# Thresholded attention on one core: two banks of a PSUM tile declared independent, and the tail's zero products in other shapes

## The chip, the core and the metric

The kernel runs on one core of a Trainium2 chip. The core has a matrix engine (PE in the profile; PEld is its loading of weights), a vector engine (DVE), an activation engine (ACT), a general engine (POOL) and a queue engine (SP) that issues DMAs. Each engine takes its instructions in the order of the program and waits on semaphores for the others. The metric is the time of one execution in device microseconds; lower is better. The median of three runs of the kernel before is 236.16 us (234.34 to 236.63).

## The reference

Q, K and V have 8 batches of 12 heads, 512 rows and 64 columns, in float32; the threshold is 0.1.

```python
scale = 1.0 / np.sqrt(Q.shape[-1])
scores = np.einsum('bhqd,bhkd->bhqk', Q, K) * scale
weights = np.exp(scores - np.max(scores, axis=-1, keepdims=True))
weights = weights / (np.sum(weights, axis=-1, keepdims=True) + 1e-10)
weights = np.where(weights > threshold, weights, 0)
weights = weights / (np.sum(weights, axis=-1, keepdims=True) + 1e-10)
return np.einsum('bhqk,bhkd->bhqd', weights, V)
```

A row of the output is zero unless one of its 512 softmax weights is above 0.1, which few rows have.

## The kernel before, in words

The kernel fills the output with zeros, looks for the rows that can have a weight above the threshold, and computes only those exactly. The 96 heads go as 48 pairs, and two pairs make a quad (24 quads, numbered q).

**The screening, for each quad.** K and Q are loaded (lines 363 to 372). PE transposes K in float32 (`do_ktr`, line 399) into two PSUM banks, and ACT or DVE copies them to SBUF (`do_kev`, lines 353 and 355); POOL casts the copy to f16 (`do_kh`, line 357). Q is cast by POOL (`do_qcast`), transposed by PE (`do_qtr`, line 425) and copied by DVE (`do_qev`, line 355). Then, for each pair of heads and each of four blocks of 128 keys, `do_sc` (line 452) makes two products, one for each head, each 128 keys by 512 queries, each filling one PSUM bank. `do_ex` turns them into f16 exponentials in SBUF: on ACT (line 461) or by a bit trick on DVE (line 463). An exponential of 512 columns takes one bank; where both banks of a pair lie side by side and one engine does both, one instruction of 1024 columns takes the two. `do_sm` (lines 483 and 494) adds the exponentials up by products with mostly zero weights, four at a time on four column groups of PE, into a PSUM bank of its own, `sum`. `do_bits` (ACT line 442, DVE line 444) and `do_norms` (line 508) do the like for the squares of Q and K, which a bound of the error needs.

**The exact part, for each of four groups of pairs** (16, 16, 12 and 4 pairs) and in seven parts x: DVE picks up to 8 candidates a row (`y`, `d`, `fl`, `mx`, `m`), PE and DVE turn them into row numbers (`ix` line 559, `qi` line 563, `qf` line 567), POOL gathers the rows of Q (`gq`), PE brings them in place (`xm` line 578), DVE masks them (`xev` lines 585 and 588), PE multiplies them with K (`xqk` line 596), ACT takes exponentials (`xexp` line 601), DVE tests them, POOL gathers a row of V (`gv`) and scatters it to the output.

**The tail.** After the last scores PE has the norms of quads 12 to 23 left (their sums go to a bank called `late`), the exact parts 4, 5 and 6, and 44 steps named `spare` (`do_spare`, line 385): products of zeros whose results nobody reads. At the very end the checks are reduced by DVE, PE and DVE (lines 802, 811 to 815), and every engine branches on one number: were a bound broken, a slow exact loop would run (line 821 on), which doesn't happen here.

**The banks.** Seven PSUM banks, numbered 0 to 6, make the ring `one`. They are allotted as three tiles of two banks each and one of one bank:

```python
banks = [psum.tile([P, min(2, pools["one"] - i), S], f32, name=f"one{i}") for i in range(0, pools["one"], 2)]
one = [banks[i // 2][:, i % 2, :] for i in range(pools["one"])]
```

So banks 0 and 1 are one tile, 2 and 3, 4 and 5, and bank 6 is alone. The framework derives the waits between engines from which instruction touched which tile before. The function `sides` gives an instruction one bank or both banks of a tile.

**The order.** `Plan.order` walks a table written out by hand, `ORDER`: one word for each of the 1395 steps, a number and a letter for its engine. For each step it takes banks (and other buffers) from the front of a list of idle ones, traces its instructions, and puts what it gives back at the end of the list. The order on each engine is therefore fixed; only the waits move. The costs and due times in the calls of `add` would serve a planner that is used when the table is empty. The steps of the tail that matter here stand at lines 730 to 736: `spare` takes a bank at its first step and gives it back at its last.

The lines that the change and the prediction touch are 351 to 357 (`copy`), 380 to 385, 391 to 433, 447 to 466, 497 to 509, 531 to 534, 557 to 602 and 730 to 736.

Of the kernel before, what the change touches and what calls it, by code (L numbers as in the profile page):

```python
# [117 lines left out]
def kernel(  # L118
# [20 lines left out]
    P = 128  # L139
# [211 lines left out]
    def copy(eng, dst, src):  # L351
        if eng == "ACT":
            nc.scalar.copy(dst, src)  # L353
        elif eng == "DVE":
            nc.vector.tensor_copy(dst, src)  # L355
        else:
            nc.gpsimd.tensor_copy(dst, src)  # L357

    def issuer(eng):
        return nc.scalar if eng == "ACTQ" else nc.sync  # L360

# [18 lines left out]
    def do_spare(eng, j):  # L380

        dst = one[at("one", "spare")]
        for c, k, m in (((0, P, 32), (32, P, 32), (64, P, 32), (96, P, 32)), ((0, D, P),),
                        ((0, D, 32), (32, D, 32), (64, D, 32), (96, D, 32)), ((0, D, P),))[j % 4]:
            nc.tensor.matmul(dst[c:c + m, :], lhsT=blank[0:k, 0:m], rhs=blank[0:k, :], start=True, stop=True)  # L385
# [5 lines left out]
    def do_ktr(eng, u):  # L391
        q, n0, k = u
        src, dst = k_b[at("k", q)], [one[at("one", ("ktr", u, i))] for i in range(2)]
        for n in range(k):
            for r in range(SO):
                for i in range(2):
                    ps = slice(i * D, (i + 1) * D)
                    c = (n * SO + r) * D
                    nc.tensor.matmul(dst[i][:, c:c + D], lhsT=src[ps, n0 + n, r, :],  # L399
                                     rhs=identity_f32[ps, ps], is_transpose=True, start=True, stop=True)  # L400
# [5 lines left out]

    def do_kev(eng, u, i, both):
# [4 lines left out]
        copy(eng, dst, src)  # L412
# [4 lines left out]
    def do_qtr(eng, u):  # L417
        q, n0, k = u
        src, dst = qh_b[at("qh", q)], [one[at("one", ("qtr", u, i))][:].bitcast(f16) for i in range(2)]
        for n in range(k):  # L420
            for r in range(SO):
                for i in range(2):
                    ps = slice(i * D, (i + 1) * D)
                    c = (n * SO + r) * D
                    nc.tensor.matmul(dst[i][:, c:c + D], lhsT=src[ps, n0 + n, r, :], rhs=identity_h[ps, ps],  # L425
                                     is_transpose=True, start=True, stop=True)

    def do_qev(eng, u, i, both):
# [4 lines left out]
        copy(eng, dst, src)  # L433
# [13 lines left out]
    def do_sc(eng, hp, t):  # L447
        q, n = divmod(hp, 2)
        qk = qk_b[at("qk", q)]
        for h in range(2):  # L450
            ps = slice(h * D, (h + 1) * D)
            nc.tensor.matmul(one[at("one", ("sc", hp, t, h))][:], lhsT=qk[ps, 1, n, t * P:(t + 1) * P], rhs=qk[ps, 0, n, :],  # L452
                             start=True, stop=True)
# [3 lines left out]
    def do_ex(eng, hp, t, h, both):  # L457
        src = sides(("sc", hp, t), h, both)
        dst = e_b[at("e", (hp, t))][:, 0 if both else h:2 if both else h + 1, :]
        if eng == "ACT":  # L460
            nc.scalar.activation(dst, src, ACTF.Exp, scale=scale, bias=-11.0 * math.log(2.0))  # L461
        else:
            nc.vector.tensor_scalar(dst.bitcast(u16), src, scale * LOG2E * 1024.0, 4096.0,  # L463
                                    op0=ALU.mult, op1=ALU.add)
# [32 lines left out]
    def do_norms(eng, q):  # L497
# [8 lines left out]
        for j in range(4):  # L506
            w = w_1 if squared[q, j // 2] else w_n
            nc.tensor.matmul(dst[32 * j:32 * j + 32, :], lhsT=w[:, c:c + 32], rhs=v[:, j // 2, j % 2, :],  # L508
# [384 lines left out]
```

## Time and profile before

| | |
|---|---|
| Runs (us) | 236.63, 234.34, 236.16; median 236.16 |
| The profiled execution | 234.87 us, of which the span from the first instruction to the last is 233.1 us |
| Busy share of the span | PE 79%, ACT 72%, DVE 64%, POOL 38% |
| Mean granted TensorE clock | 0.949 |

The profile is of one execution. A row of groups gives the line of the code, the engine, the operation, what is written and read (buffer numbers left out), the count, then busy time and mean duration of one, then the idle time of the engine before it and what ended it. In the view of waits, "DVE e L463 <- ACT e L461: 9.5, 12, 1.4" reads: before instructions of line 463 DVE sat idle for 9.5 us in 12 stretches, the longest 1.4 us, and what ended them was ACT's line 461. In the timeline a row has start and duration in us; instructions of one kind behind each other are merged ("x4"), and the idle time of the engine before stands in brackets. Matmuls are pipelined and their recorded durations include their way through the array, so that PE's busy share is not its load.

### The profile page before, as it was taken

Reading aid. Unit: us, or ns where it says so; the run is one execution under the profiler, and the core shown is the slowest. Engines: PE = TensorE matmul, PEld = TensorE weight load, DVE = VectorE, ACT = ScalarE, POOL = GpSimd, SP = SyncE. Lnnn points to the kernel's source line nnn. Section 1 sums busy time; section 2 is a strip of 40 time slices with the busy share of each in tenths; the row PEclk is TensorE's granted clock in tenths of the full one; section 3 lists DMA queues with packets and bytes.
Section 4 is the critical chain, followed back from the end, with each engine's and each line's share of the span. In section 5 each row is a group of like instructions: output and inputs, shape, how many; then the busy total and the mean of one; then the engine's idle time right before and its main releaser. Section 6 shows DMA issues by size and latency. Waiting matters only on the chain.

```text
span 233.1 us, 6162 instructions
## 1 busy us (share of the span) xinstructions
PE 184.4 (79%) x2434; PEld 71.8 (31%) x2434; DVE 150.3 (64%) x319; ACT 167.5 (72%) x242; POOL 87.8 (38%) x169
## 2 busy tenths in 40 slices
PE   6597689867687987797989798737897787798993
PEld 2233233413232333242433234311423223532220
DVE  6435478757768877686798677562585678676411
ACT  3655569757678898869889779755595989987730
POOL 4631725334133244306152532850350680323530
PEclk9979679979999999999999999976999999999997
DMA  6999760975897079708985898999920000000000
GB/s 171 271 276 293 168 180 13 275 198 151 249 284 193 3 222 239 262 3 217 300 251 143 214 321 229 247 271 379 403 115 3 0 5 0 5 6 2 6 2 6
DMA packets 70608, 38.32 MB, mean 164 GB/s; under 512 B 52020, under 2 KB 64429, under 8 KB 70576
## 3 DMA queue, kind: packets, MB, share of 16 engines
q1 hardware_dynamic: 68832, 37.10, 56.3%
q10 hardware_dynamic: 1072, 0.66, 1.0%
q8 instruction: 20, 0.33, 0.5%
q0 software_dynamic: 672, 0.13, 0.4%
q14 instruction: 12, 0.10, 0.1%
HBM read 25.62 MB, written 12.81 MB: 165 GB/s over the span
## 4 chain that ended last, share of the span: by engine, by line
PE 46%; DVE 25%; ACT 20%; issue 6%; DMA 2%; ACTq 0%; DVEq 0%
ACT e L461 17%; DVE e L463 14%; PE one L452 14%; PE sum L494 9%; PE one L385 6%; PE one L399 4%; PE one L596 4%; DVE qk L355 4%; DVE kt L355 3%; PE one L377 2%; ACT kt L353 2%; PE one L425 2%; DMA k<-in_K_dram 2%; PE sum L483 2%; PE one L508 1%
## 5 line engine op out<-in xcount | busy, mean ns | idle before, releaser
L461 ACT ACTIVATE e<-one 128x512 f16<-128x512 f32 (+1 forms) x181 | 129.4, 779 | 34.7 <-PE one L452 23.7
L463 DVE TENSOR_SCALAR e<-one 128x512 uint16<-128x512 f32 (+1 forms) x110 | 82.8, 778 | 37.7 <-PE one L452 20.8
L452 PE MATMUL one<-qk 64*128 64x512 f16 x384 | 71.3, 398 | 26.5 <-DVE e L463 14.5
L357 POOL CAST qk<-kt 128x512 f16<-128x512 f32 x46 | 28.2, 628 | 88.4 <-ACT kt L353 64.9
L494 PE MATMUL sum<-e,w_s 128*32 128x512 f16 x704 | 54.9, 400 | 2.0 <-DVE d L537 1.3
L452 PEld LDWEIGHTS <-qk 64*128 64x128 f16 x384 | 21.0, 96 | 71.2 <-issue 68.3
L357 POOL CAST qh<-q 128x512 f16<-128x512 f32 x47 | 27.7, 613 | 5.1 <-DMA q<-in_Q_dram 4.7
L353 ACT COPY kt<-one 128x512 f32<-128x512 f32 (+1 forms) x25 | 16.0, 656 | 10.5 <-DVE kt L355 5.9
L494 PEld LDWEIGHTS <-w_s 128*32 128x32 f16 x704 | 14.4, 97 | 28.6 <-issue 22.6
L399 PE MATMUL one<-identity_f,k 64*128 64x64 f32 x384 | 17.7, 234 | 6.2 <-ACT e L461 4.2
L355 DVE COPY qk<-one 128x1024 f16<-128x1024 f16 (+2 forms) x33 | 17.3, 542 | 7.3 <-PE one L425 3.0
L399 PEld LDWEIGHTS one<-identity_f,k 64*128 64x128 f32 x384 | 15.3, 144 | 12.7 <-ACT e L461 7.4
L355 DVE COPY kt<-one 128x512 f32<-128x512 f32 (+1 forms) x18 | 12.7, 717 | 9.5 <-PE one L399 6.2
L442 ACT ACTIVATE v<-qk 128x1024 bf16<-128x1024 f16 x16 | 15.9, 1047 | 2.0 <-PE one L508 2.0
L571 POOL DMA_INDIRECT qs<-in_Q_dram,idx x7 | 7.8, 1112 | 24.9 <-DVE idx L563 16.6
L385 PE MATMUL one<-blank 128*32 128x512 bf16 (+2 forms) x110 | 14.9, 386 | 0.5 <-DVE ix L567 0.5
L444 DVE TENSOR_SCALAR v<-qk 128x512 int32<-128x512 int32 x32 | 12.8, 429 | 1.6 <-PE sum L508 1.6
L425 PE MATMUL one<-identity_h,qh 64*128 64x64 f16 x384 | 10.0, 191 | 4.2 <-ACT e L461 2.0
L596 PE MATMUL one<-kt,xq 128*32 128x512 f32 x96 | 11.7, 598 | 2.0 <-ACT e L461 1.4
L425 PEld LDWEIGHTS <-qh 64*128 64x128 f16 x384 | 8.6, 95 | 10.8 <-issue 7.8
L377 PE MATMUL one<-blank,w_n 128*32 128x512 bf16 x104 | 9.3, 471 | 3.2 <-ACT e L461 1.6
L622 POOL DMA_INDIRECT vr<-in_V_dram,idx x7 | 7.7, 1104 | 7.5 <-PE one L425 4.4
(98 smaller groups left out, 103.2 us busy)
## 6 DMA issues: line engine op xcount, KB each, us to landing
out_dram<-zero SPq DMA_DIRECT2D x24, 512.0 KB
k<-in_K_dram SPq DMA_DIRECT2D x95, 128.0 KB
q<-in_Q_dram SPq DMA_DIRECT2D x23, 512.0 KB
q<-in_Q_dram ACTq DMA_DIRECT2D x2, 256.0 KB
k<-in_K_dram ACTq DMA_DIRECT2D x1, 128.0 KB
qs<-in_Q_dram,idx POOLq DMA_INDIRECT x7, 3.3
vr<-in_V_dram,idx POOLq DMA_INDIRECT x7, 3.1
out_dram<-vr,idx POOLq DMA_INDIRECT x7, 3.0
```

The lines of the kernel that those rows point to most:

```text
L353: nc.scalar.copy(dst, src)
L355: nc.vector.tensor_copy(dst, src)
L357: nc.gpsimd.tensor_copy(dst, src)
L385: nc.tensor.matmul(dst[c:c + m, :], lhsT=blank[0:k, 0:m], rhs=blank[0:k, :], start=True, stop=True)
L399: nc.tensor.matmul(dst[i][:, c:c + D], lhsT=src[ps, n0 + n, r, :], rhs=identity_f32[ps, ps], is_transpose=True, start=True, stop=True)
L425: nc.tensor.matmul(dst[i][:, c:c + D], lhsT=src[ps, n0 + n, r, :], rhs=identity_h[ps, ps], is_transpose=True, start=True, stop=True)
L442: nc.scalar.activation(dst, src, ACTF.Square)
L452: nc.tensor.matmul(one[at("one", ("sc", hp, t, h))][:], lhsT=qk[ps, 1, n, t * P:(t + 1) * P], rhs=qk[ps, 0, n, :], start=True, stop=True)
L461: nc.scalar.activation(dst, src, ACTF.Exp, scale=scale, bias=-11.0 * math.log(2.0))
L463: nc.vector.tensor_scalar(dst.bitcast(u16), src, scale * LOG2E * 1024.0, 4096.0, op0=ALU.mult, op1=ALU.add)
L494: nc.tensor.matmul(dst[32 * j:32 * j + 32, :], lhsT=w, rhs=x, start=first, stop=False, skip_group_check=True)
L596: nc.tensor.matmul(one[at("one", ("xs", x))][sl, :], lhsT=xq_b[at("xq", x)][:, n, sl], rhs=kt_b[at("kt", hp // 2)][:, hp % 2, :], start=(n ...
```

## The change

`copy` returns its instruction. A new list `users` holds, for each PSUM tile, the instructions that used it with their kind and banks. `uses` is called with every score, transpose, exponential, copy out of PSUM, zero product, late norm and product of the exact part; where an earlier one of the last 40 on the same tile is on another engine, has no bank in common with it and the pair of kinds stands in a list, it tells the framework that the two don't depend on each other. The pairs of kinds "product" with "exact" (the exact part's and the spare products with their readers), "product" with "kev", "exact" with "exact", and everything of the warm-up products of line 377 and of the tile `sum` are not in the list.

```diff
+    users = [[] for _ in banks]
+    APART = [("sc", "ex"), ("sc", "kev"), ("sc", "exact"), ("tr", "ex"), ("tr", "kev"), ("tr", "qev"), ("tr", "exact"),
+             ("ex", "ex"), ("ex", "kev"), ("ex", "qev"), ("ex", "exact"), ("kev", "kev"), ("kev", "qev"), ("qev", "qev"),
+             ("qev", "exact"), ("ex", "product"), ("qev", "product")]
+    APART = {frozenset(p) for p in APART}
+    QK = {frozenset(("sc", "qev"))}
+
+    def uses(kind, inst, first, k=1, buf=None):
+        mine = set(range(first, first + k))
+        for what, other, theirs, its in users[first // 2][-40:]:
+            both = frozenset((kind, what))
+            if not mine & theirs and other.engine != inst.ins.engine and (both in APART or (both in QK and buf != its)):
+                tc.declare_no_dep(inst.ins, other, reason="another bank, and nothing else shared")
+        users[first // 2].append((kind, inst.ins, mine, buf))
...
-            nc.tensor.matmul(one[at("one", ("sc", hp, t, h))][:], lhsT=qk[ps, 1, n, t * P:(t + 1) * P], rhs=qk[ps, 0, n, :],
-                             start=True, stop=True)
+            b = at("one", ("sc", hp, t, h))
+            uses("sc", nc.tensor.matmul(one[b][:], lhsT=qk[ps, 1, n, t * P:(t + 1) * P], rhs=qk[ps, 0, n, :], start=True,
+                                  stop=True), b, 1, at("qk", q))
...
+        uses("ex", inst, lowest(("sc", hp, t), h, both), 2 if both else 1)
```

The same call is put around the transposes ("tr"), the copies of `do_kev` and `do_qev` ("kev", "qev"), the late norms, `ix`, `xm`, `xqk` ("product"), and the reduction of the late norms, `qi`, `qf`, `xev` and `xexp` ("exact").

The second part is in `do_spare`. Before, the four steps of a cycle made 4, 1, 4 and 1 products, all in one bank; now they make 4, 8, 8 and 2, and those with 64 rows are made twice, once from the upper and once from the lower half of the rows, each half into a bank of its own. The 44 steps hold two banks instead of one.

```diff
-        dst = one[at("one", "spare")]
-        for c, k, m in (((0, P, 32), (32, P, 32), (64, P, 32), (96, P, 32)), ((0, D, P),),
-                        ((0, D, 32), (32, D, 32), (64, D, 32), (96, D, 32)), ((0, D, P),))[j % 4]:
-            nc.tensor.matmul(dst[c:c + m, :], lhsT=blank[0:k, 0:m], rhs=blank[0:k, :], start=True, stop=True)
+        quarters = [32 * c for c in range(4)]
+        for i, r, k, c, m in ([(0, 0, P, c, 32) for c in quarters], [(i, D * i, D, c, 32) for c in quarters for i in range(2)],
+                              [(i, D * i, D, c, 32) for c in quarters for i in range(2)],
+                              [(i, D * i, D, 0, P) for i in range(2)])[j % 4]:
+            b = at("one", ("spare", i))
+            uses("product", nc.tensor.matmul(one[b][c:c + m, :], lhsT=blank[r:r + k, 0:m], rhs=blank[r:r + k, :], start=True,
+                                             stop=True), b)
...
-            lambda e, j=j: do_spare(e, j), takes=[("one", "spare")] if j == 0 else [],
-            gives=[("one", "spare")] if j == SPARE - 1 else [], mode="chfh"[j % 4])
+            lambda e, j=j: do_spare(e, j), takes=[("one", ("spare", i)) for i in range(2)] if j == 0 else [],
+            gives=[("one", ("spare", i)) for i in range(2)] if j == SPARE - 1 else [], mode="ccch"[j % 4])
```

The table `ORDER` is the same.

More of the change, by code (lines that the diff above doesn't have):

```diff
@@ L405, in sides, with lowest @@
         return banks[b // 2][:, 0:2, :] if both else banks[b // 2][:, b % 2:b % 2 + 1, :]
+    def lowest(key, i, both):
+        return min(at("one", (*key, j)) for j in range(2)) if both else at("one", (*key, i))
     def do_kev(eng, u, i, both):
@@ L411, in do_kev @@
         src = sides(("ktr", u), i, both)[:, :, 0:k * SO * D].rearrange("p i (n c) -> p i n c", n=k)
-        copy(eng, dst, src)
+        uses("kev", copy(eng, dst, src), lowest(("ktr", u), i, both), m)
     def do_kh(eng, q, n):
@@ L432, in do_qev @@
         src = sides(("qtr", u), i, both).bitcast(f16)[:, :, 0:k * SO * D].rearrange("p i (n c) -> p i n c", n=k)
[L433 removed]
+        uses("qev", copy(eng, dst, src), lowest(("qtr", u), i, both), m, at("qk", q))
     squared = {}
@@ L507, in do_norms @@
             w = w_1 if squared[q, j // 2] else w_n
-            nc.tensor.matmul(dst[32 * j:32 * j + 32, :], lhsT=w[:, c:c + 32], rhs=v[:, j // 2, j % 2, :],
-                             start=first, stop=False, skip_group_check=True)
+            inst = nc.tensor.matmul(dst[32 * j:32 * j + 32, :], lhsT=w[:, c:c + 32], rhs=v[:, j // 2, j % 2, :],
+                                    start=first, stop=False, skip_group_check=True)
+            if q >= LATE:
+                uses("product", inst, at("one", "late"))
     LO, HI, ALL = slice(0, D), slice(D, P), slice(0, P)
@@ L533, in do_nm @@
         c = g if g != "late" else NG
-        nc.vector.tensor_reduce(nmax[:, c:c + 1], src, axis=AX.X, op=ALU.max)
+        inst = nc.vector.tensor_reduce(nmax[:, c:c + 1], src, axis=AX.X, op=ALU.max)
+        if g == "late":
+            uses("exact", inst, at("one", "late"))
     def do_d(eng, g):
@@ L558, in do_ix @@
         ps = rows_in(XS[x][0])
[L559 to L560 removed]
+        b = at("one", ("ix", x))
+        uses("product", nc.tensor.matmul(one[b][:, 0:1], lhsT=m_b[at("m", x)][ps, :], rhs=ones[ps, :], start=True, stop=True), b)
     def do_qi(eng, x):
[L563 to L564 removed]
+        b = at("one", ("ix", x))
+        uses("exact", nc.vector.tensor_scalar(idx_b[at("ix", x)][:, 0:1], one[b][:, 0:1], -1.0, base[:, 0, x:x + 1],
+                                     op0=ALU.mult, op1=ALU.add), b)
     def do_qf(eng, x):
[L567 to L568 removed]
+        b = at("one", ("ix", x))
+        uses("exact", nc.vector.tensor_scalar(ix_b[at("ix", x)][:], one[b][:, 0:1], -1.0, base[:, 1, x:x + 1],
+                                     op0=ALU.mult, op1=ALU.add), b)
     def do_gq(eng, x):
```

53 lines of the change are left out of this document (25 added, 28 removed).

## The prediction

> **What bounds the kernel now.** I read the page's shares first, then the view of waits, then one stretch of the timeline beside the table of steps, then the busy time in stretches of 20 us, and the tail last. The page:
>
> ```profile
> PE 184.4 (79%) x2434; PEld 71.8 (31%) x2434; DVE 150.3 (64%) x319; ACT 167.5 (72%) x242; POOL 87.8 (38%) x169
> ...
> PE 46%; DVE 25%; ACT 20%; issue 6%; DMA 2%; ACTq 0%; DVEq 0%
> ```
>
> No engine is full, and the chain that ended last changes hands between PE, DVE and ACT all the way: the three hand PSUM banks to each other, and time goes where one stands before another. DMA has 2% of the chain. So the waits between these three are what to read:
>
> ```profile
> ACT e L461 <- PE one L452: 23.7, 33, 4.7
> DVE e L463 <- PE one L452: 20.8, 27, 3.3
> PE one L452 <- DVE e L463: 14.5, 19, 1.4
> ...
> DVE e L463 <- ACT e L461: 9.5, 12, 1.4
> ACT e L461 <- DVE e L463: 9.1, 9, 3.0
> ...
> PE one L452 <- ACT e L461: 5.8, 11, 1.5
> ...
> PE one L399 <- ACT e L461: 4.2, 6, 1.9
> ```
>
> An exponential of one head needs nothing from that of another: both read their own bank and write their own half of `e`. Yet DVE's wait 12 times for ACT's and ACT's 9 times for DVE's, 9.5 + 9.1 = 18.6 us in all. The only thing that such a pair shares is the PSUM tile. That is direct evidence that waits are kept by tile and not by bank. PE's waits before scores and transposes, 14.5 + 5.8 + 4.2 = 24.5 us, are of two sorts that the view doesn't part: the bank itself is still being read, or only its neighbour is. The timeline with the banks that the table gives each step parts them:
>
> ```profile
> 59.07 0.60 ACT L461 ACTIVATE e<-one 128x512 f16<-128x512 f32 x1 [0.57 <-PE one L452]
> ...
> 59.39 0.68 DVE L463 TENSOR_SCALAR e<-one 128x512 uint16<-128x512 f32 x1
> 59.94 0.39 PE L452 MATMUL one<-qk 64*128 64x512 f16 x2
> ...
> 60.10 2.00 ACT L461 ACTIVATE e<-one 128x512 f16<-128x512 f32 x3 [0.44 <-DVE e L463]
> 60.75 0.61 PE L452 MATMUL one<-qk 64*128 64x512 f16 x4 [0.42 <-ACT e L461]
> ...
> 61.48 1.29 DVE L463 TENSOR_SCALAR e<-one 128x512 uint16<-128x512 f32 x2 [0.74 <-PE one L452]
> 61.73 0.39 PE L508 MATMUL sum<-v,w_n 128*32 128x512 bf16 x4
> ...
> 62.87 1.08 ACT L461 ACTIVATE e<-one 128x512 f16<-128x512 f32 x2 [0.76 <-DVE e L463]
> 64.00 0.71 PE L399 MATMUL one<-identity_f,k 64*128 64x64 f32 x16 [1.88 <-ACT e L461]
> 64.55 0.59 PE L452 MATMUL one<-qk 64*128 64x512 f16 x4
> 64.75 0.58 ACT L353 COPY kt<-one 128x512 f32<-128x512 f32 x1 [0.80 <-PE one L399]
> ```
>
> At 61.48 DVE reads bank 5 and then bank 1, to 62.77. ACT is free at 62.10 and wants bank 0, whose scores are there; it stands until DVE has left bank 1. ACT then reads bank 0 and bank 4, to 63.95, and only then may PE transpose K into banks 5 and 6, which DVE had left at about 62.16 (61.48 and 0.68) and ACT before 62.10. Everything behind, the copy of K at 64.75 too, is late by that.
>
> How full the engines are, stretch by stretch:
>
> ```profile
> 25.00:45.00 20.00, 17.48 (x216) 6.78 (x217) 13.94 (x24) 14.75 (x20) 9.79 (x29) 0.83 0.54 143
> 45.00:65.00 20.00, 14.44 (x204) 5.53 (x202) 12.25 (x21) 12.86 (x20) 5.78 (x11) 0.91 0.77 205
> 65.00:85.00 20.00, 17.05 (x258) 6.82 (x257) 16.30 (x25) 16.97 (x28) 8.19 (x14) 1.00 0.56 152
> 85.00:105.00 20.00, 15.80 (x202) 6.51 (x202) 15.28 (x29) 16.11 (x24) 4.60 (x6) 1.00 0.63 190
> 105.00:125.00 20.00, 17.05 (x260) 6.98 (x259) 15.30 (x28) 17.08 (x25) 8.02 (x13) 1.00 0.96 261
> 125.00:145.00 20.00, 16.90 (x242) 6.58 (x240) 15.46 (x25) 17.00 (x25) 8.30 (x16) 1.00 0.75 216
> 145.00:165.00 20.00, 13.52 (x132) 4.54 (x128) 9.54 (x20) 11.98 (x20) 7.71 (x10) 0.83 1.00 308
> 165.00:185.00 20.00, 16.04 (x232) 6.79 (x228) 12.66 (x21) 14.99 (x25) 7.76 (x15) 1.00 0.30 115
> 185.00:206.00 21.00, 17.06 (x285) 7.89 (x281) 15.67 (x25) 19.10 (x29) 9.44 (x12) 1.00 0.02 4
> ```
>
> The columns are PE, PEld, DVE, ACT and POOL, the granted clock, the DMA share and GB/s. ACT, whose durations overlap little, is the measure: 85% full in three stretches, 91% in the last, but 74, 64, 81, 60 and 75% in the others.
>
> **Part one, the declarations.** They add and remove no work: the order on each engine, the durations and the DMAs stay. What they remove is waits, and I size that twice.
>
> *By following the quoted stretch.* Without waits on the neighbour: ACT's exponential at 60.10 starts when ACT is free, 59.07 + 0.60 = 59.67, and PE's scores at 60.75 start when PE is free, 59.94 + 0.39 = 60.33; that is 0.4 us. ACT's at 62.87 starts at 62.1 less these 0.4, and PE's transposes, behind line 508's products, in the same way some 1.8 us earlier than 64.00, while ACT is still in its second exponential until 62.1 + 1.1 = 63.2 (before the 0.4). So the copy of K starts near 63.2 and not at 64.75. Together the stretch gains 1.5 + 0.4 = 1.9 us of the 0.44 + 0.42 + 0.76 + 1.88 = 3.50 us that stood there: 0.54 of it. The rest goes because two of the stalls are one behind the other. For the whole: the 18.6 us between exponentials are false throughout; of PE's 24.5 us I take half as false, 12.2. Times 0.54 that is 16.6 us. The bounds: 0.54 comes of a stretch that I chose because it shows the thing well. If a quarter comes through, 7.7 us; if all of PE's 24.5 us are false, 23.3 us.
>
> *By how full ACT is.* If the five poor stretches came to the 85% that three others reach with the same waits in them, they would last (14.75 + 12.86 + 16.11 + 11.98 + 14.99) / 0.85 = 83.2 us and not 100: 16.8 us less. At 80% all five take 88.4, 11.6 less. With all nine at 90%, 140.8 us of ACT (the sum of the column) last 156.5 instead of 181, 24.5 less.
>
> The two agree, but both lean to the high side, as true waits for banks come up behind the false ones: I take 15 us off, with 5 and 25 as the ends. In the first 25 us I take nothing: there warm-up products sit in the banks, which are not declared. What is late next: an exponential that starts earlier waits for its own scores (the 23.7 and 20.8 us rows stay as a kind), so PE's in-order issue becomes the limit. DMA can follow: the last stretch with loads in it, 145 to 165, is at a share of 1.00, but that holds the zero fills, which nobody waits for until the scatters, and 2% of the chain is DMA's.
>
> **Part two, the spare products.** They matter because in the tail PE is the chain:
>
> ```profile
> 216.78 0.60 ACT L601 ACTIVATE xe<-one 128x512 f32<-128x512 f32 x1 [1.10 <-issue]
> ...
> 217.39 3.90 ACT L442 ACTIVATE v<-qk 128x1024 bf16<-128x1024 f16 x4
> ...
> 218.15 3.62 PE L385 MATMUL one<-blank 64*128 64x512 bf16 x26
> ...
> 225.79 0.40 PE L508 MATMUL one<-v,w 128*32 128x512 bf16 x4
> 226.02 0.39 PE L385 MATMUL one<-blank 128*32 128x512 bf16 x4
> 226.24 0.39 PE L508 MATMUL one<-v,w 128*32 128x512 bf16 x4
> 226.56 2.32 PE L385 MATMUL one<-blank 64*128 64x512 bf16 x16
> 228.81 0.38 PE L811 MATMUL one<-identity_f,okm 128*1 128x128 f32 x2
> ```
>
> The 16 products from 226.56 are the last 7 steps: (2.32 - 0.39) / 6 = 0.32 us a step, and each differs in shape from its neighbours. Where the shape stays (225.79, 226.02, 226.24) a step takes 0.22. So a change of shape costs 0.10 us and the number of products in a step nothing, as four run side by side. In the new cycle two of four neighbours have one shape. Counted along PE's table from the step before the first spare product to the last, 54 changes of shape become 44; behind the sixteenth step, where PE never stands, 28 become 21. That is 0.7 us off the end.
>
> A step of 8 products has no row. Its bound from below: both halves of the rows run side by side, as in the score rows quoted above (four products in 0.59 us, two halves twice: 0.59 - 0.39 = 0.20 a pair), and it takes 0.22. From above: the halves go one behind the other, 0.44. How fast PE can issue is told by
>
> ```profile
> 197.30 1.49 PE L483 MATMUL sum<-e,w_s 128*32 128x256 f16 x48
> ```
>
> ```profile
> L483 PE MATMUL sum<-e,w_s 128*32 128x256 f16 (+1 forms) x128 | 4.7, 274 | 0.1
> ```
>
> 48 products in 1.49 us, 0.27 of it the last one's way through (the mean of the group in the second row), so 0.026 us each, and 8 in 0.21, no more than a step. I take 0.22, because the halves' overlap is shown and only the narrower columns are not.
>
> The second bank has a price. With one idle bank less, the table now gives `xs` of parts 4, 5 and 6 all bank 3 and `xm` all bank 4; each is read before the next needs it by the rows' times. But the spare products now hold banks 0 and 2, and bank 2 shares a tile with bank 3; products and readers of the exact part are not declared. `xexp` of part 6, at 216.78 now, is traced behind the sixteenth spare step, so it will wait for that, until about 219, and the spare step behind the next waits for it: 0.3 us on PE. The squares of ACT (line 442) move back by 2.2 us with it; the last two end near 225.8 instead of 224.2, and the norms that use them stand in PE's table near 226.2, so this just stays hidden. Were it not, it would cost up to 1.5 us. Sum of part two: -0.7 + 0.3 = -0.4 us; ends -1 and +6.3 (the 22 steps of 8 at 0.22 more each, 4.8, and the 1.5).
>
> **The sum** against the profiled execution: 234.87 (span 233.1 and 1.8 around it) - 15 - 0.4 = 219.5. The median of the runs, 236.16, stood 1.3 above that execution, so 220.8 for the median.
>
> **The rivals.**
>
> *True waits fill the gaps.* The order is fixed, and the bank that PE or ACT wants may be freed hardly earlier than its neighbour. Then only a part of the 18.6 us between exponentials comes through, say a quarter, 4.7 us: 231. For it: waits for scores, 44.5 us, are the largest rows and remain. Against it: the stretch at 59 to 65, where the true releases are 0.4 to 1.8 us earlier.
>
> *The clock.* At 25 to 45, 45 to 65 and 145 to 165 the granted clock is 0.83, 0.91 and 0.83, and inside it falls to half:
>
> ```profile
> 28.00:32.00 4.00, 4.00 (x35) 1.38 (x36) 1.65 (x4) 2.21 (x4) 1.61 (x3) 0.50 0.63 175
> ```
>
> That is (0.17 + 0.09 + 0.17) x 2 x 20 = 17.2 us at half, and PE's busy share in the three is 0.76. If the dips come of PE's standing about and go with it, up to 17.2 x 0.76 / 2 = 6.5 us more are saved: 214. Against it: other stretches with waits show 1.00. The Trainium skill, "TensorE: Matmul & The Clock Gate", section "What's actually happening", says that the clock falls to half after an idle window of about 3.4 us and returns after as long a busy one; by that rule denser work would do away with the dips, and this trace agrees so far as they lie in the stretches where ACT and PE are emptiest.
>
> *The declarations do nothing*, if the waits that remain ask for something just as late. Then 236.16 - 0.4 = 235.8. Against it: the followed stretch, where all that is really needed is there earlier.
>
> *The spare products cost more than the body gives: slower.* If the row halves of the narrow steps don't overlap, the tail grows by 4.8 us. It decides where the body gains less than that; with a body refilled by true waits to a gain of 1 us, 236.16 - 1 + 4.8 = 240.
>
> **How the numbers follow.** Forecast (215 to 227) 0.60; true waits (227 to 233) 0.16; the clock (209 to 215) 0.12; nothing 0.06; slower 0.06. The likeliest is 220.8. The range from 209 to 233 leaves out the last two and slips at its ends. A measurement of this kernel can tell about 1% from no change, 2.4 us here: faster 0.87 (the first three, less 0.01), same 0.07, slower 0.06.
>
> **What would show it.** Right: the rows of exponentials that wait for exponentials of the other engine gone, or down from 18.6 to under 4 us; PE's waits before lines 452 and 399 for exponentials down by about half; ACT at 85% or more in most stretches before the tail; the tail's start near 191 (206 less 15); two score rows of ACT and DVE side by side on one tile with unchanged 0.60 and 0.68 us. In the tail, steps of 8 products at 0.22 beside a like step, `xexp` of part 6 behind the sixteenth spare step, and the last spare product 0.4 us earlier after the tail's start. Wrong: the 18.6 us still there; or gone with the waits for scores grown by as much; or DMA rows in the chain; or PE's last products spread over more than 0.32 us a step.

## The result, and the profile after

The changed kernel takes 189.33 us (median of 4 runs, 189.28 to 190.75), the kernel before on the same chip 236.39 us (4 runs, 234.34 to 236.89). The ratio is 0.8037, with a 95% interval of 0.7976 to 0.8097. (Some executions run at a lower granted clock and take longer; the times in this document are medians of all executions, the ratios compare the faster ones alone.) The forecast was 220.8 us, with a range from 209 to 233: the direction was right, the size was not, by a factor of three. 47 us went, and 15.4 were forecast.

The page of after, its busy shares and the granted clock in 40 slices. (In the lines of after, scores are L475, exponentials L484 on ACT and L486 on DVE, K's transposes L418, Q's L447, spare products L403, norms L532, the copies of K and Q L353 on ACT and L355 on DVE, and the exponentials of the exact part L635.)

```profile
PE 171.0 (91%) x2566; PEld 70.3 (38%) x2566; DVE 146.7 (78%) x319; ACT 162.3 (87%) x242; POOL 87.4 (47%) x169
...
PEclk9999999999999999999999999999999999999998
```

The work is the same (ACT 162.3 us against 167.5, DVE 146.7 against 150.3), and it lies closer together. The clock is full in all slices but the last (0.997 on the mean). The view of waits of after, the rows that answer to those quoted before:

```profile
DVE e L486 <- PE one L475: 5.3, 8, 2.3
ACT e L484 <- PE one L475: 4.9, 8, 1.5
...
PE one L475 <- ACT e L484: 1.4, 4, 0.4
...
DVE e L486 <- ACT e L484: 1.3, 2, 0.7
...
PE one L475 <- DVE e L486: 0.8, 1, 0.8
```

Exponentials waiting for exponentials of the other engine: from 18.6 us to 1.5 (1.3 in the row above, and 0.2 on ACT). Scores waiting for exponentials: from 20.3 to 2.2. And the rows that the prediction expected to "stay as a kind", exponentials waiting for their scores: from 44.5 us to 10.2. The busy time by stretches (the columns as in the prediction):

```profile
25.00:45.00 20.00, 19.84 (x308) 8.77 (x306) 19.50 (x35) 19.53 (x29) 12.50 (x29) 1.00 0.87 218
45.00:65.00 20.00, 19.81 (x308) 8.52 (x310) 19.65 (x34) 19.65 (x34) 8.82 (x16) 1.00 1.01 278
65.00:85.00 20.00, 18.68 (x272) 7.94 (x269) 17.09 (x35) 19.30 (x29) 7.23 (x12) 1.00 0.76 221
85.00:105.00 20.00, 19.91 (x284) 8.11 (x287) 19.12 (x33) 19.55 (x31) 9.71 (x18) 1.00 0.97 265
105.00:125.00 20.00, 19.04 (x281) 8.06 (x281) 17.66 (x35) 19.60 (x29) 11.77 (x18) 1.00 1.02 305
125.00:145.00 20.00, 19.87 (x290) 7.69 (x291) 15.14 (x26) 19.39 (x35) 10.79 (x19) 1.00 0.93 320
145.00:160.00 15.00, 13.68 (x239) 7.13 (x234) 13.22 (x23) 15.00 (x23) 6.66 (x10) 1.00 0.02 4
```

ACT, the fourth busy time, is 96 to 100% full in every stretch (132.0 of 135 us), where it was 60 to 91% full before. That is close to the ceiling of the body: with ACT's work as it is, some 3 us are left to win in these 135.

The first 25 us, where the prediction took nothing off, gained too. First before, then after:

```profile
0.00:25.00 25.00, 16.90 (x234) 7.01 (x234) 13.10 (x60) 12.76 (x17) 10.34 (x38) 0.93 0.99 252
```

```profile
0.00:25.00 25.00, 17.86 (x272) 7.72 (x273) 14.55 (x63) 15.56 (x21) 12.00 (x47) 1.00 0.93 240
```

ACT has done 15.56 us of work there and not 12.76, so it is 2.8 us ahead when the 25 us are over. The tail's start and end, first before, then after:

```profile
205.48 0.81 PE L385 MATMUL one<-blank 128*32 128x512 bf16 x5
```

```profile
159.96 0.82 PE L403 MATMUL one<-blank 128*32 128x512 bf16 x12
...
174.49 2.15 PE L403 MATMUL one<-blank 64*32 64x512 bf16 x39 [0.18 <-ACT xe L635]
...
176.79 3.68 PE L403 MATMUL one<-blank 128*32 128x512 bf16 x66
...
181.16 2.15 PE L403 MATMUL one<-blank 64*32 64x512 bf16 x40
182.20 0.17 DVE L836 TENSOR_REDUCE okm<-oks 128x1 f32<-128x16 f32 x1
183.25 0.38 PE L845 MATMUL one<-identity_f,okm 128*1 128x128 f32 x2
```

The first spare product came 45.5 us earlier (205.48 to 159.96). From there to the last two products of PE it took 228.81 - 205.48 = 23.33 us before and 183.25 - 159.96 = 23.29 after. All of the gain lies ahead of the tail (45.5 of the 45.6 us between the two spans, 233.1 and 187.5), and the second part of the change moved nothing that these two executions show.

How the gain grows is seen by following ACT, whose order is the same in both kernels. The stretch that the prediction followed ended with a copy of K at 64.75; a copy of `sum` (line 527, in after 553) comes behind four more copies of K. Before and after:

```profile
55.00 0.58 ACT L353 COPY kt<-one 128x512 f32<-128x512 f32 x1 [0.96 <-DVE kt L355]
...
83.92 0.59 ACT L527 ACTIVATE y<-sum 64x512 f32<-64x512 f32 x1
```

```profile
42.37 0.59 ACT L353 COPY kt<-one 128x512 f32<-128x512 f32 x1
...
45.75 3.47 ACT L484 ACTIVATE e<-one 128x512 f16<-128x512 f32 x6 [0.19 <-PE one L475]
49.05 0.64 ACT L353 COPY kt<-one 128x512 f32<-128x512 f32 x1
...
65.01 0.59 ACT L553 ACTIVATE y<-sum 64x512 f32<-64x512 f32 x1
```

The copy at 55.00 came 12.6 us earlier, the one at 64.75 by 15.7, the copy of `sum` at 83.92 by 18.9, the tail by 45.5. The gain is spread over the whole body but not evenly: it grows fastest where ACT was emptiest before. Between the exponential at 59.07 (the first of the six at 45.75) and the copy of K lay 5.68 us before and 3.30 after. The prediction followed just this stretch and came to 3.78. So the local reading was right, even a little low; what went wrong came after it.

### The profile page after: what moved, and what is told of

The parts are those of the page before. It is cut to its first block, busy times and chain, and to the rows that moved or that the text cites. A ratio compares the mean times of both kernels' runs of the same rounds, so it can differ in the third digit from the quotient of the medians.

```text
span 187.5 us, 6445 instructions
## 1 busy us (share of the span) xinstructions
PE 171.0 (91%) x2566; PEld 70.3 (38%) x2566; DVE 146.7 (78%) x319; ACT 162.3 (87%) x242; POOL 87.4 (47%) x169
## 4 chain that ended last, share of the span: by engine, by line
PE 58%; ACT 22%; DVE 8%; issue 6%; DMA 3%; SPq 1%; ACTq 0%; DVEq 0%
PE one L475 18%; ACT e L484 17%; PE sum L518 15%; PE one L629 6%; PE one L418 6%; PE one L403 4%; DMA k<-in_K_dram 3%; PE one L447 3%; ACT v L464 2%; DVE qk L355 2%; PE one L393 2%; DVE e L486 2%; ACT kt L353 2%; DVE kt L355 1%; PE sum L507 1%
## 5 line engine op out<-in xcount | busy, mean ns | idle before, releaser
L484 ACT ACTIVATE e<-one 128x512 f16<-128x512 f32 (+1 forms) x181 | 126.1, 801 | 6.1 <-PE one L475 4.9
L486 DVE TENSOR_SCALAR e<-one 128x512 uint16<-128x512 f32 (+1 forms) x110 | 81.6, 776 | 8.3 <-PE one L475 5.3
L475 PE MATMUL one<-qk 64*128 64x512 f16 x384 | 64.7, 380 | 4.2 <-ACT e L484 1.4
L518 PE MATMUL sum<-e,w_s 128*32 128x512 f16 x704 | 52.1, 384 | 1.3 <-DVE d L565 1.3
L475 PEld LDWEIGHTS <-qk 64*128 64x128 f16 x384 | 20.1, 94 | 41.5 <-issue 36.7
L355 DVE COPY qk<-one 128x1024 f16<-128x1024 f16 (+2 forms) x33 | 17.3, 541 | 4.9 <-PE one L447 2.0
L418 PE MATMUL one<-identity_f,k 64*128 64x64 f32 x384 | 16.6, 227 | 1.2 <-DMA k<-in_K_dram 1.1
L353 ACT COPY kt<-one 128x512 f32<-128x512 f32 (+1 forms) x25 | 16.1, 680 | 1.5 <-PE one L418 1.4
L601 POOL DMA_INDIRECT qs<-in_Q_dram,idx x7 | 7.8, 1113 | 19.9 <-DVE idx L592 19.6
L418 PEld LDWEIGHTS one<-identity_f,k 64*128 64x128 f32 x384 | 14.8, 140 | 5.8 <-ACT e L484 2.2
L355 DVE COPY kt<-one 128x512 f32<-128x512 f32 (+1 forms) x18 | 12.6, 713 | 4.9 <-ACT xe L635 2.4
L403 PE MATMUL one<-blank 64*32 64x512 bf16 (+2 forms) x242 | 14.5, 383 | 0.7 <-DVE ix L597 0.5
L466 DVE TENSOR_SCALAR v<-qk 128x512 int32<-128x512 int32 x32 | 12.7, 427 | 0.5 <-PE sum L532 0.4
L447 PEld LDWEIGHTS <-qh 64*128 64x128 f16 x384 | 8.9, 95 | 7.7 <-issue 4.6
L393 PE MATMUL one<-blank,w_n 128*32 128x512 bf16 x104 | 8.7, 446 | 3.1 <-DVE w_n L226 1.6
L447 PE MATMUL one<-identity_h,qh 64*128 64x64 f16 x384 | 10.3, 191 | 1.3 <-DVE e L486 0.5
```

Source lines behind the costliest of these rows:

```text
L353: return nc.scalar.copy(dst, src)
L355: return nc.vector.tensor_copy(dst, src)
L403: uses("product", nc.tensor.matmul(one[b][c:c + m, :], lhsT=blank[r:r + k, 0:m], rhs=blank[r:r + k, :], start=True, stop=True), b)
L418: uses("tr", nc.tensor.matmul(dst[i][:, c:c + D], lhsT=src[ps, n0 + n, r, :], rhs=identity_f32[ps, ps], is_transpose=True, start=True, sto ...
L447: uses("tr", nc.tensor.matmul(dst[i][:, c:c + D], lhsT=src[ps, n0 + n, r, :], rhs=identity_h[ps, ps], is_transpose=True, start=True, stop= ...
L475: uses("sc", nc.tensor.matmul(one[b][:], lhsT=qk[ps, 1, n, t * P:(t + 1) * P], rhs=qk[ps, 0, n, :], start=True, stop=True), b, 1, at("qk", q))
```

## The experiments

The theory after the result: all of the gain is waits that were kept by the tile of two banks and not by the bank, and the prediction missed kinds of pairs, and took for true some waits that were the echo of false ones. The rivals: the clock, which is full now; the spare products; and that only an order of steps made for banks that are apart can gain so much. Each ratio is to the kernel before on the same chip in the same set; "95%" stands for the interval.

### The two parts of the change by themselves

The declarations with the old spare products (in `do_spare` the old products go through `uses("product", ...)` with their one bank, the 44 steps take one bank again):

```diff
-        quarters = [32 * c for c in range(4)]
-        for i, r, k, c, m in ([(0, 0, P, c, 32) for c in quarters], ...
+        dst = one[at("one", "spare")]
+        for c, k, m in (((0, P, 32), (32, P, 32), (64, P, 32), (96, P, 32)), ((0, D, P),),
...
```

> Part one alone: the declarations as in the changed kernel, the spare products as before (4, 1, 4 and 1 in one bank, 110 in all). If the declarations make the whole gain: 189.3 to 190.3 us. If the new spare products, which make PE denser in the tail, had a share in it beyond the 0.4 us forecast: over 191.

193.29 us (192.45 to 195.32), ratio 0.8261, 95% 0.811 to 0.8412.

The other half: the kernel before with the new spare products alone, on two banks and not declared.

> Part two alone: the spare products in the new shapes and two banks, no declarations. By the forecast's working the tail gets 0.7 us shorter through fewer changes of shape and 0.3 longer through the wait of the sixteenth step: 236 us, within 1 us of before. If steps of 8 cost twice: about 241.

236.98 us, ratio 1.0056, 95% 0.9987 to 1.0125: nothing that can be told from no change. The whole change once more, on the chip of three runs of the next sections (the two pairs around exponentials together, all but exponentials with exponentials, and the first run of one-bank tiles):

> The changed kernel again, on the chip of this call, as the yardstick: 189 to 192 us. Against it stands the kernel with the declarations alone, whose ratio to before was 0.826 and not 0.804: if the new spare products have a share, this one's ratio is near 0.804 again; if that was the chip, near 0.826.

193.83 us (193.44 to 195.42), ratio 0.8287, 95% 0.8194 to 0.838. By its expectation the first of these three runs spoke for a share of the spare products, as it lay over 191 us; but the whole change came no lower here. So the declarations alone are the change, and the spare products are worth nothing that a run can tell. The 4 us between this run and the first result are the chip or the set, not the kernel (see the last section).

### Which pairs it was

`APART` in the changed kernel lists the kinds of pairs that are declared independent. Five runs cut the list. Exponentials with exponentials alone, and scores with exponentials alone:

```diff
-    APART = [("sc", "ex"), ("sc", "kev"), ...
+    APART = [("ex", "ex")]
...
-    QK = {frozenset(("sc", "qev"))}
+    QK = set()
```

> The changed kernel with one pair of kinds declared, exponential with exponential. Theory of the sum (each kind of wait gives what stands in its own rows, 18.6 us at about half or all): 218 to 227. Theory of the echo (lateness goes round between PE, ACT and DVE, and PE's waits before scores, still by tile, hold the others on the same beat): under 8 us of gain, 228 to 235.

> The changed kernel with one pair of kinds declared, scores with exponentials. Theory of the sum: PE's 20.3 us of waits before scores, half to all: 216 to 226. Theory of the echo: exponentials still wait for each other on one tile, so the gain is clearly less than the 47 us less what e3 gives; 215 to 228. What e3 and e4 gain together against 47 us tells: much less than 47 is the echo, about 47 the sum.

The first gave 227.07 us (ratio 0.9664, 95% 0.9578 to 0.975), the second 224.05 us (0.9579, 0.9432 to 0.9725). Their views of waits, first with exponentials apart from each other, then with scores apart from exponentials:

```profile
ACT e L482 <- PE one L473: 23.3, 31, 4.4
...
DVE e L484 <- PE one L473: 19.9, 30, 2.4
```

```profile
ACT e L482 <- DVE e L484: 12.4, 14, 2.2
...
DVE e L484 <- PE one L473: 11.3, 14, 2.4
DVE e L484 <- ACT e L482: 9.3, 11, 1.3
ACT e L482 <- PE one L473: 8.9, 18, 1.1
```

In the first, the 18.6 us of waits between exponentials are gone but for 2.4, and the time fell by 8: the waits for scores stayed at 43.2 us, as the prediction's rival of true waits would have it. In the second the waits for scores fell from 44.5 to 20.2 us, though no wait of an exponential for its own score was touched. The declaration also frees an exponential from a score in the neighbour's bank; but where the trace of before is followed with the banks that the table gives, only some 5 of the 44.5 us are of that sort, and the others end with the exponential's own score. So most of the 24.3 us were an echo: the exponential was late because its score was late, and the score was late because PE stood before a neighbour's bank. (Followed in the same way, some 16 of PE's 24.5 us were for the neighbour's bank alone.) The two together (`APART = [("sc", "ex"), ("ex", "ex")]`):

> The changed kernel with two pairs of kinds declared: exponential with exponential and scores with exponentials. Alone they gave ratios of 0.966 and 0.958 to before. Theory of the sum: 0.966 x 0.958 = 0.925, about 219 us. Theory of the echo: more together than one after the other, well under 215 us; the transposes and copies, still by tile, keep it above the changed kernel's 189 to 191.

215.93 us (213.66 to 216.91), ratio 0.9231, 95% 0.9143 to 0.9319. The product of the two alone is 0.9664 x 0.9579 = 0.926: they add up and no more. These are the pairs that the prediction's sum is about, but for PE's transposes behind exponentials (4.2 us), and they gave 18.7 us, close to the 16.6 that it worked out. Another 22 to 28 us are missing. What waits remain in this kernel:

```profile
DVE e L484 <- PE one L473: 11.2, 12, 2.5
ACT e L482 <- PE one L473: 11.1, 18, 1.5
DVE kt L355 <- PE one L416: 6.9, 4, 4.4
...
ACT kt L353 <- DVE kt L355: 4.2, 6, 1.1
PE one L416 <- ACT e L482: 3.9, 7, 1.0
```

ACT's copy of K still waits 6 times for DVE's copy of K, which reads another bank and writes another half; and K's transposes wait for exponentials. The opposite cut, everything that has to do with the transposes and the copies of K and Q (and the exact part) and neither of the two pairs above:

```diff
-    APART = [("sc", "ex"), ("sc", "kev"), ...
-             ("ex", "ex"), ("ex", "kev"), ...
+    APART = [("sc", "kev"), ...
+             ("ex", "kev"), ...
```

> The kernel after, without the declarations score-exponential and exponential-exponential. If the kinds of pairs multiply, as the two exponential pairs did with each other, it comes to 0.8287/0.9231 = 0.898 of before, some 211 us. If the transposes and copies only count once the exponentials are apart, 0.95 or more (224 us or more). If they are the main cause by themselves, 200 us or less.

213.66 us (212.43 to 215.91), ratio 0.9084, 95% 0.9012 to 0.9155: 21.6 us. So the copies and transposes by themselves are worth at least as much as the two pairs around the exponentials, and 0.9231 x 0.9084 = 0.839 for the two groups comes near to what the whole change gives (0.8037 to 0.8287). And all but exponentials with exponentials:

> The changed kernel with all pairs declared but exponential with exponential. Theory of the sum: it loses what that pair gave alone, 8 us: 197 to 199. Theory of the echo: one kind left by tile holds the others on its beat, so it loses much more than 8 us: over 202.

206.36 us (205.86 to 207.23), ratio 0.8801, 95% 0.8722 to 0.888. In its view of waits

```profile
ACT e L484 <- DVE e L486: 11.0, 12, 3.2
...
DVE e L486 <- ACT e L484: 9.1, 13, 2.5
```

the 20.1 us between exponentials cost 12.5 us on one chip (206.36 against 193.83), where taking them alone out of the kernel before had given 8 and where they had stood at 18.6 us. A false wait is worth more when the others are gone; that nothing else hides it then is the likely reason.

### The tile by itself

No declaration, the old spare products, and the seven banks as seven tiles. An exponential, or a copy, of two banks becomes two instructions.

```diff
-    banks = [psum.tile([P, min(2, pools["one"] - i), S], f32, name=f"one{i}") for i in range(0, pools["one"], 2)]
-    one = [banks[i // 2][:, i % 2, :] for i in range(pools["one"])]
+    banks = [psum.tile([P, 1, S], f32, name=f"one{i}") for i in range(pools["one"])]
+    one = [banks[i][:, 0, :] for i in range(pools["one"])]
...
-                both = after[i] == self.ids[twin] and ...
+                both = False
```

> The kernel before with seven PSUM tiles of one bank and no declaration; instructions that took two banks of a tile are split in two. If the shared tile is the whole cause, the waits go as with the declarations, and the cost is that of the split: 74 exponentials of ACT of 1024 columns at 1.03 us become 148 at 0.60, +12.6 us of ACT, 19 of DVE at 1.22 become 38 at 0.69, +3 us: 195 to 206. If the declarations do something else than part the banks (a shorter wait for anything else): over 215.

> One-bank tiles, no declarations, the spare steps of before, once more beside the two others of this set: 189 to 191 us (ratio 0.81).

189.84 us (189.49 to 190.11), ratio 0.8098, 95% 0.8027 to 0.817, and on another chip 191.56 us, 0.816, 0.8113 to 0.8208. That is all of the gain without one declaration: the shared tile is the cause. I had put the price of splitting instructions higher. Two exponentials of 512 columns behind each other take 1.08 us on ACT and 1.29 us on DVE (the rows at 62.87 and 61.48 in the prediction); one of 1024, in the groups of before by shape (busy time, then mean ns of one):

```profile
L461 ACT ACTIVATE e<-one 128x1024 f16<-128x1024 f32 x74 | 74.0, 1030 | 7.8 <-PE one L452 7.1 <-ACT e L461 0.3
...
L463 DVE TENSOR_SCALAR e<-one 128x1024 uint16<-128x1024 f32 x19 | 23.2, 1221 | 8.2 <-PE one L452 6.8 <-ACT e L461 1.4
```

So 0.05 us on ACT and 0.07 on DVE for each split.

Two runs asked why one-bank tiles were 4 us ahead of the declarations on one chip. The first splits the instructions but keeps tiles and declarations (`both = False` in the changed kernel); the second names the kinds of pairs that `APART` left out:

```diff
-             ("qev", "exact"), ("ex", "product"), ("qev", "product")]
+             ("qev", "exact"), ("ex", "product"), ("qev", "product"),
+             ("exact", "product"), ("exact", "exact"), ("kev", "product"), ("kev", "exact")]
```

> The kernel after, with every instruction that reads two banks at once split in two of 512 columns. If the 4 us between one-bank tiles (189.84) and the declarations (193.83) are the two-bank instructions, which need both of their banks free at once, this comes to 189 to 191 us. If they are the pairs that no declaration names, it stays at 193 to 196 us, the splits costing 0.05 us each.

> The kernel after, with the missing kinds of pairs named too: exact steps with products and with each other, K's copies with products and with exact steps. If the 4 us that one-bank tiles are ahead are these pairs, 189 to 190 us (ratio 0.81). If not, 193 to 194 us (0.83).

The first gave 197.21 us (ratio 0.8384, 95% 0.8338 to 0.843), slower than either and outside both ranges, which I had not expected and which its profile didn't explain. The second gave 188.36 us (0.8036, 0.7991 to 0.8081), but on another chip than the run at 193.83, and the change as made gives 0.8069 on a third, so the times alone don't tell. The traces tell more. One-bank tiles part the warm-up products of line 377 too, which no declaration names. The first 25 us with the declarations (the run at 193.83) and with one-bank tiles (189.84), on one chip:

```profile
0.00:25.00 25.00, 18.10 (x274) 7.81 (x274) 14.95 (x64) 15.95 (x21) 12.27 (x48) 1.00 0.95 251
```

```profile
0.00:25.00 25.00, 21.77 (x342) 9.68 (x342) 19.18 (x75) 19.76 (x39) 14.72 (x53) 1.00 0.94 241
```

ACT's exponential behind its first 20 banks starts at 19.8 us with one-bank tiles and at 23.6 with the declarations, a lead of 3.8 us. Four rows of waits on or of the warm-up products, 5.4 us in all, stand in the view of the first and not in that of the second. The splits then take a part of it back (ACT is busy for 166.8 us and not 162.9), and the first spare product comes 1.0 us earlier, 161.52 against 162.50. From there to the last two products of PE it takes 22.45 us against 25.50, the other 3 of the 4 us. About 1 us of that fits the missing pairs: in the profile of the second run `xexp` of part 6 no longer stands behind the sixteenth spare step,

```profile
170.09 0.60 ACT L636 ACTIVATE xe<-one 128x512 f32<-128x512 f32 x1 [0.29 <-ACT v L465]
```

and its tail takes 21.88 us, against 23.28 in the change as made on the third chip. With 17 spare steps left out as well (last section of the experiments) the pairs add nothing: 18.56 us, and 18.72 with one-bank tiles. The other 2 us of the run at 193.83 are the same kernel's (25.50 against 23.28), and no pair's.

### The clock

The kernel before with more zero products in the pairs of heads where the granted clock dipped. They are added to the sums and change nothing in them:

```diff
+        if hp in CLOCK:
+            for n in range(2):
+                for j in range(4):
+                    nc.tensor.matmul(dst[32 * j:32 * j + 32, :], lhsT=blank[:, 0:32], rhs=blank[:], start=False, stop=False,
+                                     skip_group_check=True)
```

> The kernel before, with each score product's eight zero-weight products added again (they add nothing to the sums) in the heads 0 to 11 and 32 to 39, the stretches in which the granted clock dipped to a half. No declaration. If the dips are a cause of their own, holding the clock gives back the 4 to 6 us of half clock that the windows of before show: 230 to 232 us. If the dips only follow from PE standing before banks, the added products find room in PE's idle time but nothing else moves, or they push: 236 to 241 us. In neither case does the clock explain 47 us.

255.96 us, ratio 1.0927, 95% 1.0854 to 1.1, far above both ranges. The two stretches that had 0.83 and 0.91 before:

```profile
25.00:45.00 20.00, 17.77 (x294) 7.57 (x293) 11.75 (x21) 12.70 (x17) 9.74 (x31) 1.00 0.45 116
45.00:65.00 20.00, 17.87 (x314) 7.99 (x312) 11.26 (x19) 11.90 (x17) 6.85 (x12) 1.00 0.61 164
```

```profile
PE 212.9 (84%) x3074; PEld 86.3 (34%) x3074; DVE 150.0 (59%) x319; ACT 168.7 (66%) x242; POOL 87.8 (35%) x169
```

The clock was held, and ACT was emptier than before (12.7 and 11.9 of 20 us). But PE's busy time grew by 28.5 us (from 184.4 to 212.9), and the kernel by 20: the added products stood on the path, so this run doesn't say what the clock alone is worth. The cuts of `APART` say more. With the two pairs around exponentials the mean granted clock is 0.992 in the profiled execution (0.983 and 0.984 in the others), with the transposes and copies alone 0.991, and they take 215.93 and 213.66 us. With a clock that is all but full, 22 us and more of the gain are still missing (215.93 against 193.83 on one chip): the clock doesn't explain them.

### The order of the steps

The table written out by hand is emptied (`ORDER = ""`), so that the planner's simple pass orders the steps; once in the kernel before, once in the changed one.

> The kernel before with the hand-written order taken out, so that the planner's own simple pass orders the steps. It says nothing by itself: the base for the next. A guess: 240 to 300 us.

> The same simple order with the declarations and the spare steps of after. If the size of the gain comes from the tiles whatever the order, its ratio to the simple order without declarations is 0.77 to 0.85. If it comes from an order made for banks that are apart, it gains less: 0.90 to 1.0.

273.88 us and 230.93 us: ratios of 1.1648 (95% 1.1561 to 1.1735) and 0.9853 (0.9792 to 0.9914) to the kernel before, so 0.9853 / 1.1648 = 0.846 from the one to the other, with ends of 0.834 and 0.858 from the ends of the two intervals. A poorer order gains 43 us, nearly as much, so the gain doesn't need an order made for banks that are apart. The clock hardly moved here, from a mean of 0.925 to 0.937 in the executions at 273 us to 0.951 to 0.959, which speaks against it once more.

### Fewer spare products

In the profile after, PE's last two products at 183.25 have what they need at 182.37 (182.20 and 0.17) and stand behind the last spare products in PE's order. Two kernels leave out 17 of the 44 spare steps (16 to 19, 24 to 29, 37 to 43), products of zeros that nobody reads: with one-bank tiles, and with the declarations and the missing pairs. The second ran beside the change as made.

```diff
+        if j in LEFT_OUT:
+            return
...
+    LEFT_OUT = {16, 17, 18, 19, 24, 25, 26, 27, 28, 29} | set(range(37, 44))
```

> One-bank tiles, and 17 of the 44 spare steps of the tail left out (zero products that nobody reads: steps 16 to 19, 24 to 29 and 37 to 43). In the profile after, the exponential of part 6 stood behind the 16th spare step, and the end waited 0.9 us for the last spare steps. If the tail is set by PE's queue, it loses 2 to 3 us: 187 to 188 us. If the spare steps only fill waits, it stays at 190 us; if leaving them out lets the clock fall, it goes above 191 us.

> The kernel after with the missing kinds of pairs named, and 17 of the 44 spare steps of the tail left out (16 to 19, 24 to 29, 37 to 43; zero products that nobody reads). If the two gains add up (188.36 against 189 to 194, and 191.56 to 186.7 with one-bank tiles): 183 to 185 us, ratio 0.78, the fastest of all. If either only filled what the other empties, 186 to 189 us.

> The change as made, on the same chip as the run beside it: 189 to 194 us, ratio 0.80 to 0.83.

With one-bank tiles 186.7 us (185.74 to 189.24; ratio 0.7954, 95% 0.7893 to 0.8015) beside 191.56 for all the steps: 4.9 us, more than the 2 to 3 expected. With declarations 185.13 us (184.09 to 185.69; 0.7865, 0.7826 to 0.7905) beside 189.23 (188.99 to 190.84; 0.8069, 0.8028 to 0.8111). The last is the fastest of all: 4.1 us below the change as made, on one chip, with intervals that lie apart. The two gains don't add up. Its end:

```profile
179.08 0.17 DVE L840 TENSOR_REDUCE okm<-oks 128x1 f32<-128x16 f32 x1
179.31 0.38 PE L849 MATMUL one<-identity_f,okm 128*1 128x128 f32 x2 [1.18 <-DVE okm L840]
```

PE now waits 1.18 us for DVE's `okm`, where it came too late for it before. At the pace of the rows of after, (3.68 - 0.39) / 11 = 0.30 us a step, 17 steps are 5.1 us; what is measured is a little less, as DVE takes over at the end. The clock was 0.999 in this run: these products weren't needed for it.

## Why the prediction was wrong

**What bounds the kernel: right.** PE, DVE and ACT did stand before banks that were free, by the tile; one-bank tiles show it without any declaration.

**The followed stretch: right, if a little low.** 5.68 us less 1.9 was forecast, 3.30 was measured.

**From the stretch to the whole: wrong, and this is the step that failed.** The prediction put the false waits at "the 18.6 us between exponentials" and half of "PE's 24.5 us", 30.8 us, and took 0.54 of it. Three things were missing in that sum.

First, kinds of pairs. It had read the page for exponentials and scores. ACT's copies of K waiting for DVE's copies of K are as plainly false as exponentials waiting for each other, and the view of waits of before has the row:

```profile
ACT kt L353 <- DVE kt L355: 5.9, 6, 1.9
```

The declarations that go with transposes and copies gave 21.6 us by themselves, the two pairs around exponentials 18.7. The sum of 16.6 us was nearly right for the second group, and stood for the whole.

Second, the echoes. That "the 23.7 and 20.8 us rows stay as a kind" was false: 10.2 of these 44.5 us are left, and scores apart from exponentials took 24.3 off alone. A wait for something that is needed is still no true cost, if what is waited for was itself held up by a false wait. The prediction used the rows of waits as prices, and such a row names only the last link. The half that it took of PE's 24.5 us, 12.2, was less of a fault: some 16 were for the neighbour's bank alone.

Third, the first 25 us. "In the first 25 us I take nothing", as the warm-up products aren't declared: 2.8 us came off there all the same (ACT's work there went from 12.76 to 15.56 us). That these products hold the others up was right: one-bank tiles, which free them, were another 3.8 us ahead.

**The second sizing: its ceiling was wrong.** It filled ACT to 85% because three stretches of before stood there "with the same waits in them", and gave 24.5 us for 90%. But 85% was what the false waits allowed. ACT came to 97.8% (132.0 of 135 us). The same row sum that the prediction had, 140.8 us of ACT in 181, would have given 181 - 140.8 / 0.978 = 37 us off; ACT's shorter busy time (167.5 to 162.3) gives another 5 of the 45.5; the last 3 lie in the first 25 us. That "both lean to the high side, as true waits for banks come up behind the false ones" turned the correction the wrong way.

**The range** followed the same step: its low end, 209, was that of the rival of the clock, and the first part's own bound was 25 us. No case stood for ACT nearly full.

**The rivals.** True waits: shown wrong, though a cut with one kind of pair alone looks just like it (8 us from 18.6). The clock: it went to 1.00 as this rival had it. The trace agrees with the Trainium skill ("TensorE: Matmul & The Clock Gate", "What's actually happening") in that denser work did away with the dips, here and in the kernel with added products. But kernels with the clock at 0.99 are still 22 us behind, so it is a small part at most. How small was not settled. That the dips lay where PE was emptiest held for two of the three stretches: in 25 to 45 its busy time was 17.48 us, the highest of the nine, though with fewer products (216) than in most.

**The spare products: small, as forecast.** -0.4 us was forecast, 23.33 to 23.29 was measured, in one execution each. `xexp` of part 6 does stand behind the sixteenth spare step (and PE 0.18 us behind it, for the 0.3 that was forecast):

```profile
173.75 0.60 ACT L635 ACTIVATE xe<-one 128x512 f32<-128x512 f32 x1 [3.44 <-issue]
```

A step was forecast at 0.27 us on the mean (two of four with a change of shape, 0.32, and two without, 0.22). It takes 0.30. If a change still costs 0.10, the steps of 8 products take 0.28 each, between the bounds of 0.22 and 0.44 and near the lower.

## What to carry to other kernels

Where several engines share a PSUM tile of two banks, look for one wait that can only be the tile's (two readers of different banks), and then count all waits among all users of those tiles as suspect, those for true inputs too. The size is not the sum of the rows. Here it came near to how far the fullest engine was from full, its busy time over about 0.98; but that is a bound and no rule, as in the simple order 43 us went with ACT busy for only 70% of the span at the end. Tiles of one bank do the same as a list of declarations that must name each kind of pair, at 0.05 to 0.07 us for each instruction that has to be split.

## What the runs showed of the hardware that was not expected

The same changed kernel gave ratios of 0.8037, 0.8287 and 0.8069 on different chips or in different sets, and the intervals of the last two don't meet. The traces of these two are 0.02 us apart at 119 us and then part, first the one with 193.83 us, then the one with 189.23:

```profile
119.09 0.39 PE L475 MATMUL one<-qk 64*128 64x512 f16 x2
...
120.09 0.69 DVE L355 COPY qk<-one 128x1024 f16<-128x1024 f16 x1 [1.71 <-PE one L475]
120.15 1.73 ACT L484 ACTIVATE e<-one 128x512 f16<-128x512 f32 x3 [0.79 <-PE one L475]
...
120.84 0.39 PE L475 MATMUL one<-qk 64*128 64x512 f16 x2 [1.36 <-issue]
```

```profile
118.73 0.69 DVE L355 COPY qk<-one 128x1024 f16<-128x1024 f16 x1 [0.31 <-PE one L447]
...
119.11 0.75 PE L475 MATMUL one<-qk 64*128 64x512 f16 x4
```

DVE's copy of Q has its transposes in both at 118.4 and starts 1.36 us later in the first; PE, ACT and DVE all stand for a moment, and nothing in the profile says for what. (Between 105 and 125 us ACT does 17.2 to 18.1 us of work in six of the ten profiles of the changed kernel and its near relatives, and 19.6 in the other four.) Another 2.2 us are lost in the tail of the first, from the first spare product to the last two products of PE (25.50 us against 23.28), most of it while PE goes through spare products more slowly than in the second. DMA's share between 100 and 120 us is 1.04 there, at 309 GB/s; but the profile of the first result has 1.03, at 313 GB/s, and no such pause. What it is stays open. It shows that ratios from different chips or sets can differ here by 3% (0.8037 and 0.8287), so that less than that can be told only from runs beside each other, or from the traces.
